# 24 column tiles of block 1's input projection multiplied ahead of the chain, in pairs by one level of a Strassen-type algorithm

## The chip, the core and the metric

The kernel runs on one core of a Trainium2 chip. The metric is the time of one execution on the device in microseconds (us), as the median of several runs. A core has five engines that run side by side: PE (TensorE, the matrix array), DVE (VectorE), ACT (ScalarE), POOL (GpSimd) and SP (SyncE, which here only issues DMA transfers). Each engine works through its own list of instructions in order, and an instruction that waits holds up all that stands behind it on the same engine. A scheduler decides, when the kernel is built, in which order each engine's list is written.

## The reference, cut to what matters

There are two blocks of a network on one sequence of 1024 tokens with 1024 features. The change lies in block 1 alone:

```python
shift, scale, gate = split(silu(c) @ w_mod + b_mod)
hx = rmsnorm(x, norm_g) * (1 + scale) + shift           # [1024, 1024]
q, k, v, zA, lr, uB, zB, gA, gB = split(hx @ w_in)      # one big projection
o  = gated_linear_attention(q, k, v, decays(lr), s0)    # s0 from 256 context tokens, 4 heads, two directions
yA = (rmsnorm(o) * silu(zA)) @ w_branch_a
yB = (pool(uB) * silu(zB)) @ w_branch_b                 # pool: differences of window sums, 4 groups
x  = x + gate * ((sigmoid(gA) * yA + sigmoid(gB) * yB) @ w_out)
```

Block 2 (attention with 16 heads and a feed-forward part) follows and is the same in both kernels.

## The kernel before, in words

Activations lie features first, in 8 tiles of 128 x 1024. Every product is made in three passes: each operand is split into a high and a low part (`split`: a cast on ACT, a subtraction on DVE or POOL), and `mm3` (lines 235 to 238) issues low x high, high x low, high x high as three matmuls of 128 x 512. For a weight tile `load` (line 226) reads 256 KB into `wraw` on SP's queue, ACT casts it to `whi` (line 190) and POOL subtracts to get `wlo` (line 182).

The front loads x, sums its squares, makes shift and scale by `mod` (a product with w_mod, a copy `row` on ACT, then four small products with `sel` that turn the row into columns `modv`), and forms the normed input in `hh`/`hl`: for each feature tile, x times scale on DVE, hh on ACT (line 423), hl on DVE. `gemm_late` starts the first two q products with feature tiles 0 to 3, while tiles 4 to 7 are still being made.

The projection is cut into column tiles: q, k, v, lr, and 40 "z" tiles (`proj_z`): 8 each of ub, zb, za, gb and ga. One z tile is 2 halves of tokens x 8 feature tiles x 3 = 48 matmuls, then for zb, za, gb, ga a sigmoid of three ACT functions on each half (lines 222 to 224). Results go to DRAM.

The attention chain `gla_head` runs for 4 heads: prefix sums of the decays (`X`, with small products `wup`), seven levels of scores (`EQ`, `EK`, `Q` with `kx`; mostly DVE work), a chain of states (each step: a transposition of `kh` with `ident`, a copy `kt` on DVE, a product `v,kt`, an update `sx` on DVE), then the outputs (`osq`, `rr`, `ya`). Between heads stand the `pool_group`s: `pool_tile` makes window sums `win` of u on DVE and splits them to `dh`/`dl`, a small product follows, and `zb` is multiplied in and stored to `yb_d`. Pool groups 0 and 1 follow heads 1 and 2, groups 2 and 3 both follow head 3.

`weave` puts the projection's column tiles as fillers before the 122 steps of that chain, evenly. So PE works on a filler while DVE and ACT work on the chain. After the chain, `load_split` (line 786) reads `yb_d` back as `raw` through three `ld` buffers and splits it to `rh`/`rl` for the branch products.

## Time and profile before

| what | value |
| --- | --- |
| median of three runs | 2676.07 us (2675.43 to 2678.48) |
| span of the profiled execution | 2679.3 us, mean granted TensorE clock 0.985 |
| PE busy | 2549.1 us (95%), 14390 matmuls |
| DVE busy | 1505.9 us (56%) |
| ACT busy | 961.0 us (36%) |
| POOL busy | 809.5 us (30%) |
| part with front and woven chain | 0 to about 873 us |

The profiled execution has no time of its own beside its span. Busy shares are means over stages of different kinds: the first 873 us hold the chain and its fillers, the rest is branch products and block 2. A granted clock of 1.00 is 2.4 GHz, 0.50 is 1.2 GHz.

### The profile page before, as it was taken

To read this page: it belongs to the slowest core of one execution; us is meant where nothing else is said; L and a number is where in the kernel's file an instruction comes from. 1 tells how busy PE (TensorE), PEld (TensorE's weight loads), DVE (VectorE), ACT (ScalarE), POOL (GpSimd) and SP (SyncE) were. 2 spreads that over 40 slices of the span, in tenths; PEclk is the share of its full clock that TensorE was granted. 3 is DMA by queue.
4 is the path that set the end of the run, shared out by engine and by line. 5 is a ranking of instruction groups with operands and counts; after the bars stand their busy time and mean duration, and the time that the engine had idled before them with its cause. 6 is when DMAs were issued, how large, how long until landed. Compare 5 with 4: busy or idle time off the path is not lost. (4 is left out here: it accounts for less than half of the span.)

```text
span 2679.3 us, 36279 instructions
## 1 busy us (share of the span) xinstructions
PE 2549.1 (95%) x14390; PEld 2015.2 (75%) x14390; DVE 1505.9 (56%) x2190; ACT 961.0 (36%) x1634; POOL 809.5 (30%) x592
## 2 busy tenths in 40 slices
...
GB/s 256 125 74 108 86 158 85 151 111 101 145 80 146 196 193 110 118 103 155 127 127 127 113 77 114 124 105 28 40 49 49 48 48 48 47 48 48 48 48 75
DMA packets 109113, 270.55 MB, mean 101 GB/s; under 512 B 13600, under 2 KB 18592, under 8 KB 108944
## 3 DMA queue, kind: packets, MB, share of 16 engines
...
## 5 line engine op out<-in xcount | busy, mean ns | idle before, releaser
L182 POOL TENSOR_TENSOR wlo<-wraw,whi 128x512 fp32r<-128x512 f32 (+1 forms) x363 | 537.3, 1482 | 1639.2 <-ACT whi L190 1593.1
L190 ACT CAST whi<-wraw 128x512 fp32r<-128x512 f32 (+1 forms) x363 | 223.8, 617 | 709.4 <-PE pp L238 617.6
L236 PE MATMUL pp<-hl,whi 128*128 128x512 f32 (+1 forms) x768 | 312.1, 407 | 4.8 <-DVE hl L185 4.8
L237 PE MATMUL pp<-hh,wlo 128*128 128x512 f32 (+1 forms) x768 | 307.2, 400 | 0.4 <-POOL wlo L182 0.4
L238 PE MATMUL pp<-hh,whi 128*128 128x512 f32 (+1 forms) x768 | 306.4, 399 | 0.0
L238 PE MATMUL pp<-u3h,whi 128*128 128x512 f32 x688 | 271.4, 395 | 0.0
L237 PE MATMUL pp<-u3h,wlo 128*128 128x512 f32 x688 | 271.0, 394 | 0.0
L236 PE MATMUL pp<-u3l,whi 128*128 128x512 f32 x688 | 270.2, 393 | 0.0
L182 DVE TENSOR_TENSOR x<-x,pp 128x512 f32<-128x512 f32 (+1 forms) x184 | 121.5, 664 | 208.5 <-PE pp L238 208.5
L236 PEld LDWEIGHTS pp<-hl,whi 128*128 128x128 f32 (+1 forms) x768 | 144.9, 189 | 42.5 <-DVE hl L185 5.8
L237 PEld LDWEIGHTS pp<-hh,wlo 128*128 128x128 f32 (+1 forms) x768 | 144.8, 189 | 38.9 <-issue 6.1
L238 PEld LDWEIGHTS pp<-hh,whi 128*128 128x128 f32 (+1 forms) x768 | 144.9, 189 | 33.7 <-issue 0.4
L1028 DVE COPY pt<-pg 128x512 f32<-128x512 f32 (+2 forms) x192 | 101.0, 553 | 92.5 <-PE pg L1026 91.8
L237 PEld LDWEIGHTS pp<-u3h,wlo 128*128 128x128 f32 x688 | 129.0, 188 | 30.9
L236 PEld LDWEIGHTS pp<-u3l,whi 128*128 128x128 f32 x688 | 129.2, 188 | 30.3
L238 PEld LDWEIGHTS pp<-u3h,whi 128*128 128x128 f32 x688 | 129.1, 188 | 30.1
L236 PE MATMUL pp<-fl,whi 128*128 128x512 f32 (+1 forms) x368 | 142.0, 386 | 0.0
L238 PE MATMUL pp<-fh,whi 128*128 128x512 f32 (+1 forms) x368 | 141.4, 384 | 0.0
L237 PE MATMUL pp<-fh,wlo 128*128 128x512 f32 (+1 forms) x368 | 140.8, 383 | 0.0
L185 DVE SCALAR_TENSOR_TENSOR t<-p,vec,t 128x1023 f32<-128x1023 f32 x88 | 122.1, 1395 | 33.1 <-ACT t L1144 32.1
L237 PE MATMUL pp<-uh,wlo 128*128 128x512 f32 x336 | 139.2, 414 | 0.0
L236 PE MATMUL pp<-ul,whi 128*128 128x512 f32 x336 | 138.3, 412 | 0.0
(384 smaller groups left out, 5434.0 us busy)
## 6 DMA issues: line engine op xcount, KB each, us to landing
...
```

Source lines behind the costliest of these rows:

```text
L182: return (eng or nc.vector).tensor_tensor(out=o, in0=a, in1=b, op=op)
L185: return (eng or nc.vector).scalar_tensor_tensor(out=o, in0=a, scalar=s, in1=b, op0=op0, op1=op1)
L190: nc.scalar.copy(hi, src)
L236: nc.tensor.matmul(ps, ah, bl, start=first, stop=False)
L237: nc.tensor.matmul(ps, al, bh, start=False, stop=False)
L238: nc.tensor.matmul(ps, ah, bh, start=False, stop=last)
L1028: nc.vector.tensor_copy(o, ps[:, :w])
```

## The change

24 of the 40 z tiles (ub, zb, ga) are taken out of the fillers and multiplied before the chain starts. Two column tiles ct and ct+4 make a pair; with the two halves of features and the two halves of tokens a pair is a 2 x 2 by 2 x 2 block product, and it is made with 7 products instead of 8 (Winograd's form). Such a product is 4 feature tiles x 3 = 12 matmuls of 128 x 512. The sums of weights (`up_sum`) are formed on DVE, the sums of the normed input (`t_sum`, `t_parts`) once, on DVE, ACT and POOL, and they stay resident for all 12 pairs. `up_result` combines the products on DVE and ACT, and accumulates two of them in a bank with others where that serves.

All of this stage is pinned: the scheduler must leave it in the order in which it is written, on each engine. The stage has its own memory pools; new pools are opened after it, and the loads of the context, of the tables and of the first q weights come from them. The weave then has 31 fillers and two small ones instead of 55 and two.

```diff
-NSLOT, NF, NT, NLD, NH, NQT = 32, 3, 2, 3, 5, 5
+NSLOT, NFIRST, NF, NT, NLD, NH, NQT = 32, 16, 3, 2, 3, 5, 5
...
+PROJ = [(n, ct) for n in ("ub", "zb", "ga") for ct in range(4)]
+REST = [n for n in ("za", "gb", "ga") if (n, 0) not in PROJ]
+SEVEN = (1, 6, 2, 5, 7, 3, 4)
+EARLY = (1, 5, 2, 6, 7, 3, 4)
...
+    def pin(ins):
+        return tc.keep_in_program_order(ins) if pinned[0] else ins
...
-    get = psum_pool(es, pp=(HALF, 3), pg=(HALF, 5))
+    get = psum_pool(es, pp=(HALF, 8))
+    size["h"] = ("e", N_E)
...
+    wm = {blk: mod_load(blk, row) for blk in (1, 0)}
+    bank_rstd(acc, r)
...
+    def up_load(q):
+        n, ct = PROJ[q]
+        raws[q] = []
+        for c in (ct, ct + 4):
+            for j in range(2):
+                raws[q].append(seg("wr", "wr"))
+                dma(raws[q][-1], io[f"w_{n}"][c, j])
+    def up_sum(q, n):
+        a11, a12, a21, a22 = raws[q]
+        if (q, n) in sums:
+            return
+        if n in (5, 6):
+            sums[q, 5], sums[q, 6] = seg("s1", "ws"), seg("s2", "ws")
+            tt(sums[q, 5], a21, a22, ALU.add)
+            tt(sums[q, 6], sums[q, 5], a11, ALU.subtract)
+        elif n == 3:
+            sums[q, 3] = sums[q, 6]
+            tt(sums[q, 3], a12, sums[q, 6], ALU.subtract)
+        elif n == 7:
+            tt(a11, a11, a21, ALU.subtract)
+            sums[q, 7] = a11
+        else:
+            sums[q, n] = raws[q][{1: 0, 2: 1, 4: 3}[n]]
+    def up_parts(q, n):
+        wh, wl = seg("wh", "w", F32R), seg("wl", "w", F32R)
+        split(sums[q, n], wh, wl, nc.gpsimd)
+        wparts[q, n] = [x.rearrange("p (k c) -> p k c", k=4) for x in (wh, wl)]
...
+    def up_product(q, n):
+        wh, wl = wparts.pop((q, n))
+        key = {1: 1, 2: 1, 7: 7, 4: 7}.get(n, 6)
+        first = (q, key) not in banks
+        if first:
+            banks[q, key] = get("pp")
+        ps = banks[q, n] = banks[q, key]
+        for j in range(4):
+            th, tl = T[n][j]
+            mm3(ps, wh[:, j], wl[:, j], th, tl, first and j == 0, j == 3, True)
...
+    def up_result(q, n):
+        if q not in outs and n in (2, 7):
+            outs[q] = row("o"), row("o")
+        p, v = outs.get(q, (None, None))
+        b = banks[q, n]
+        u1 = part.get((q, 1))
+        if n == 1:
+            part[q, 1] = seg("p1", "e")
+            copy(part[q, 1], b)
+        elif n == 2:
+            copy(p[:, LOW], b)
+        elif n == 7:
+            tt(v[:, HIGH], part[q, "v"], b, ALU.add)
+        elif n == 3:
+            tt(p[:, HIGH], u1, b, ALU.add)
+        elif n == 4:
+            tt(v[:, LOW], part[q, "u"], b, ALU.add)
...
+    def up_rest(q, i):
+        n, ct = PROJ[q]
+        if i == 6:
+            for c, o in zip((ct, ct + 4), outs[q]):
+                dma(z_d[n][c], o)
+        if n == "ub" or i > 3:
+            return
+        x = outs[q][i // 2][:, (LOW, HIGH)[i % 2]]
+        if n == "zb":
+            o = seg("s", "e")
+            sigmoid(x, o)
+            tt(x, x, o, ALU.mult)
+        else:
+            sigmoid(x, x)
...
+    T = {n: [(hh[j + k0][:, half], hl[j + k0][:, half]) for j in range(4)] for n, k0, half in ((1, 0, LOW), (2, 4, LOW), (3, 4, HIGH))}
...
+    def normed(k):
+        pin(nc.vector.tensor_scalar(g1s[:, k], modv[:, KD + k], 1.0, V("norm_g", k), op0=ALU.add, op1=ALU.mult))
+        x, sh = xt[k], modv[:, k, 0:1]
+        stt(x, x, g1s[:, k, 0:1], r, ALU.mult, ALU.mult)
+        act(hh[k], x, AF.Identity, bias=sh)
+        stt(hl[k], x, sh, hh[k].bitcast(F32), ALU.add, ALU.subtract)
...
+    def t_parts(n, j):
+        src = {5: xt[j][:, LOW], 7: xt[j][:, HIGH], 6: xt[j + 4][:, HIGH], 4: xt[j + 4][:, LOW]}[n]
+        t = row("T", F32R)
+        split(src, t[:, LOW], t[:, HIGH], nc.gpsimd if j % 2 else None)
+        T[n].append((t[:, LOW], t[:, HIGH]))
+    early = [(q, n) for n in EARLY for q in range(2)]
+    order = early + [(q, n) for q in range(2, len(PROJ)) for n in SEVEN]
...
+    for b in range(2):
+        mod(2 * b + 1, modv[:, KD + 4 * b : KD + 4 * b + 4], wm[2 * b + 1], tag="pp")
+        mod(2 * b, modv[:, 4 * b : 4 * b + 4], wm[2 * b], tag="pp")
+        pinned[0] = True
+        if b == 0:
+            wm = {blk: mod_load(blk, row) for blk in (3, 2)}
+            for q in range(2):
+                up_load(q)
+        else:
+            tt(dsh, modv[:, 4:8, 0], modv[:, :4, 0], ALU.subtract)
+        for k in range(4 * b, 4 * b + 4):
+            normed(k)
+        for j in range(4 - 4 * b):
+            t_sum(5, j)
+            t_parts(5, j)
+        for s in range(2 * b, 2 * b + 2):
+            up_sum(*early[s])
+            up_parts(*early[s])
+    for s, (q, n) in enumerate(order):
+        i = s - 14 if s < 14 else s % 7
+        if s:
+            up_result(*order[s - 1])
+        for n_, at in ((6, 1), (7, 3), (4, 6)):
+            for j in range(2 * (s - at), 2 * (s - at) + 2):
+                if 0 <= j < 4:
+                    if n_ == 6:
+                        t_sum(7, j)
+                    if n_ != 7:
+                        t_sum(n_, j)
+                    t_parts(n_, j)
+        nxt = 2 if s == 8 else q + 1 if i == 0 and q + 1 < len(PROJ) else 0
+        if nxt:
+            up_load(nxt)
+        if s + 4 < len(order):
+            up_sum(*order[s + 4])
+        if s and s + 3 < len(order):
+            up_parts(*order[s + 3])
+        if q > 2:
+            up_rest(q - 1, i)
+        elif q == 2:
+            for q_ in range(2):
+                up_rest(q_, i)
+        up_product(q, n)
+    up_result(*order[-1])
+    for i in range(7):
+        up_rest(len(PROJ) - 1, i)
+    pinned[0] = False
+    es.close()
+    front.close()
+    front = ExitStack()
+    wpool, sb = main_pools(front, NFIRST)
+    es = ExitStack()
+    get = psum_pool(es, pp=(HALF, 3), pg=(HALF, 5))
+    state = {"gla": None}
+    hch, hcl, xct = [], [], []
+    rc, accc = qt("rc", w=LC), b1k("accc")
+    for i in range(2):
+        xct.append(b1k(f"xc{i}"))
+        nc.sync.dma_start(xct[i].rearrange("p (k t) -> p k t", k=4), ctxT[4 * i : 4 * i + 4].rearrange("k p t -> p k t"))
...
-    wm = {blk: mod_load(blk, b1k) for blk in (1, 0)}
-    wq = [load(io["w_qk"][h, i], 4, P) for h in range(2) for i in range(2)]
-    bank_rstd(acc, r)
-    for b in range(2):
-        mod(2 * b + 1, modv[:, KD + 4 * b : KD + 4 * b + 4], wm[2 * b + 1], last[1] if b else None)
-        mod(2 * b, modv[:, 4 * b : 4 * b + 4], wm[2 * b], last[3] if b else None)
-        if b == 0:
-            wm = {blk: mod_load(blk, b1k) for blk in (3, 2)}
-            for i in range(2):
-                xct.append(b1k(f"xc{i}"))
-                nc.sync.dma_start(
-                    xct[i].rearrange("p (k t) -> p k t", k=4), ctxT[4 * i : 4 * i + 4].rearrange("k p t -> p k t")
-                )
-        for k in range(4 * b, 4 * b + 4):
-            nc.vector.tensor_scalar(g1s[:, k], modv[:, KD + k], 1.0, V("norm_g", k), op0=ALU.add, op1=ALU.mult)
-            x, sh = xt[k], modv[:, k, 0:1]
-            stt(x, x, g1s[:, k, 0:1], r, ALU.mult, ALU.mult)
-            hh.append(b1k(f"hh{k}", F32R))
-            hl.append(b1k(f"hl{k}", F32R))
-            last.append(nc.scalar.activation(hh[k], x, AF.Identity, bias=sh))
-            stt(hl[k], x, sh, hh[k].bitcast(F32), ALU.add, ALU.subtract)
...
-    qb = gemm_late([wq[:2], wq[2:]], hh, hl, tags=['pg', 'pp'], k0=4)
     context()
-    fill = [(("q", h), lambda h=h: proj_q(h, qb[h])) for h in range(2)]
+    fill = [(("q", h), lambda h=h: proj_q(h)) for h in range(2)]
...
-    fill += [((n, c), lambda n=n, c=c: proj_z(n, c)) for c in range(KD) for n in ("ub", "zb")]
-    fill += [((n, c), lambda n=n, c=c: proj_z(n, c)) for n in ("za", "gb", "ga") for c in range(KD)]
+    fill += [((n, c), lambda n=n, c=c: proj_z(n, c)) for n in REST for c in range(KD)]
...
-        fill.insert(16 + 16 * b, (("gate", b), lambda b=b: gate_x(b)))
+        fill.insert(12 + 6 * b, (("gate", b), lambda b=b: gate_x(b)))
     fill = [(k, max(0, CH1 * (n - 3) // (len(fill) - 3)), f) for n, (k, f) in enumerate(fill)]
...
     es.close()
-
-    # branch products and the merge
+    front.close()
+    hold.close()
+    wpool, sb = main_pools(ctx, NSLOT)
```

**The front.** On DVE, at the start of the program: x is scaled (the rows `x<-x,g1s,r`, 128x1024), then hl is taken. Before:

```order
L185 SCALAR_TENSOR_TENSOR x_4_237<-x_4_237,g1s,r_275 128x1024
L185 SCALAR_TENSOR_TENSOR x_5_240<-x_5_240,g1s,r_275 128x1024
L185 SCALAR_TENSOR_TENSOR x_7_245<-x_7_245,g1s,r_275 128x1024
L185 SCALAR_TENSOR_TENSOR x_9_250<-x_9_250,g1s,r_275 128x1024
L185 SCALAR_TENSOR_TENSOR hl_64_394<-x_4_237,modv,hh_63_393 128x1024
L185 SCALAR_TENSOR_TENSOR hl_66_400<-x_5_240,modv,hh_65_399 128x1024
L182 TENSOR_TENSOR modv<-pg_426,vec 128x8
L418 TENSOR_SCALAR g1s<-modv,vec 128x2
L185 SCALAR_TENSOR_TENSOR hl_68_406<-x_7_245,modv,hh_67_405 128x1024
L185 SCALAR_TENSOR_TENSOR hl_70_412<-x_9_250,modv,hh_69_411 128x1024
```

and of the change, the first two feature tiles, and then the place where tile 4 follows on tile 3:

```order
L207 SCALAR_TENSOR_TENSOR x_3_236<-x_3_236,g1s,r_274 128x1024
L207 SCALAR_TENSOR_TENSOR hl_320<-x_3_236,modv,hh_312 128x1024
L521 TENSOR_SCALAR g1s<-modv,vec 128x2
L207 SCALAR_TENSOR_TENSOR x_4_239<-x_4_239,g1s,r_274 128x1024
L207 SCALAR_TENSOR_TENSOR hl_321<-x_4_239,modv,hh_313 128x1024
```

```order
L204 TENSOR_TENSOR T_419<-x_6_244,T_419 128x512
L204 TENSOR_TENSOR x_8_249<-x_8_249 128x512
L204 TENSOR_TENSOR modv<-pp_445,vec 128x8
L204 TENSOR_TENSOR modv<-pp_462,vec 128x8
L204 TENSOR_TENSOR dsh<-modv 128x4
L521 TENSOR_SCALAR g1s<-modv,vec 128x2
L207 SCALAR_TENSOR_TENSOR x_10_254<-x_10_254,g1s,r_274 128x1024
L207 SCALAR_TENSOR_TENSOR hl_324<-x_10_254,modv,hh_316 128x1024
```

Before, four scalings stood together ahead of the four subtractions; now each subtraction (which needs ACT's hh of the same tile) stands directly behind its scaling. The rows for tiles 4 to 7 stand behind the sums for operand T and behind both modv of the second pair of w_mod blocks. On PE the first products stand in the same way behind both of these w_mod blocks; the last rows of `mod` (line 413) and the first product:

```order
L413 MATMUL pp_445<-sel,row_443 128x2 x4
L402 MATMUL pp_451<-wm_370,st_81 32x512 x2
L402 MATMUL pp_451<-wm_372,st_81 32x512 x2
L402 MATMUL pp_451<-wm_374,st_81 32x512 x2
L402 MATMUL pp_451<-wm_376,st_81 32x512 x2
L413 MATMUL pp_462<-sel,row_460 128x2 x4
L268 MATMUL pp_501<-hl_320,wh_426 128x512
L269 MATMUL pp_501<-hh_312,wl_427 128x512
L270 MATMUL pp_501<-hh_312,wh_426 128x512
L268 MATMUL pp_501<-hl_321,wh_426 128x512
```

Before, the first product of tile 0 stood ahead of the last w_mod block, and tiles 0 to 3 and then 4 to 7 followed each other in one product.

**Behind the last Winograd-type product.** SP's queue of the change, where the stores of ga end and the loads for context, tables and q weights follow (`o` are the results of the last two pairs):

```order
L216 DMA ga_d_146<-o_2128 128x1024
L216 DMA ga_d_150<-o_2129 128x1024
L216 DMA ga_d_147<-o_2275 128x1024
L216 DMA ga_d_151<-o_2276 128x1024
L607 DMA xc_426_2368<-in_ctxT 128x4x256
L607 DMA xc_427_2370<-in_ctxT 128x4x256
L645 DMA cosT_2399<-in_con 128x1024
L646 DMA sinT_2400<-in_con 128x1024
L262 DMA wraw_2426<-in_w_qk 128x512
L262 DMA wraw_2432<-in_w_qk 128x512
```

and before, where these loads stood in the first 40 rows of the queue, behind w_mod alone:

```order
L350 DMA wm_385<-in_w_mod 128x1024
L414 DMA xc_61_387<-in_ctxT 128x4x256
L414 DMA xc_62_389<-in_ctxT 128x4x256
L428 DMA edge<-in_con 128x64
L437 DMA cosT_500<-in_con 128x1024
L438 DMA sinT_501<-in_con 128x1024
L231 DMA wraw_654<-in_w_lr 128x384
L231 DMA wraw_660<-in_w_lr 128x384
L231 DMA wraw_749<-in_w_qk 128x512
L231 DMA wraw_755<-in_w_qk 128x512
```

The PE rows at this place are the last product with T, the sum over the squares of the context (`accc,ones`), and the first q product:

```order
L269 MATMUL pp_2299<-T_678,wl_2279 128x512
L270 MATMUL pp_2299<-T_678,wh_2278 128x512
L618 MATMUL pg_2378<-accc_2367,ones 128x256
L268 MATMUL pp_2438<-hl_320,whi_2427 128x512
L268 MATMUL pp_2464<-hl_320,whi_2427 128x512
L269 MATMUL pp_2438<-hh_312,wlo_2428 128x512
L270 MATMUL pp_2438<-hh_312,whi_2427 128x512
```

All loads of the next stage moved from the start of the queue to a place behind the stores of this stage's last results.

**The end of the chain.** PE before, at the last pool group's product (`dl`, `dh`) and behind it:

```order
L237 MATMUL pg_7900<-dh_7799,wlo_7805 128x512
L238 MATMUL pg_7900<-dh_7799,whi_7804 128x512
L236 MATMUL pg_7908<-dl_7800,whi_7804 128x512
L237 MATMUL pg_7908<-dh_7799,wlo_7805 128x512
L238 MATMUL pg_7908<-dh_7799,whi_7804 128x512
L236 MATMUL pp_7958<-hl_64_394,whi_7919 128x512
L237 MATMUL pp_7958<-hh_63_393,wlo_7920 128x512
```

and of the change:

```order
L270 MATMUL pg_8288<-dh_8268,whi_8273 128x512
L268 MATMUL pg_8299<-dl_8269,whi_8273 128x512
L269 MATMUL pg_8299<-dh_8268,wlo_8274 128x512
L270 MATMUL pg_8299<-dh_8268,whi_8273 128x512
L268 MATMUL pg_8307<-dl_8269,whi_8273 128x512
L269 MATMUL pg_8307<-dh_8268,wlo_8274 128x512
L270 MATMUL pg_8307<-dh_8268,whi_8273 128x512
L268 MATMUL pp_8602<-rl_8541,whi_8591 128x512
```

Before, 216 further filler matmuls (with `hl`, `hh`) stood between the last `dl` product and the first branch product (`rl`, `rh`); now the branch products follow directly. Between the last `osq` product of head 3 and the last `dl` product there are 207 filler matmuls before and 76 now. In the same way PE has, between the last score product of a head (`Q,kx`) and the first transposition of its state chain (`ident,kh`), 3, 49 and 34 filler matmuls for heads 1, 2 and 3 before, and none now. SP's queue of the change at the same place:

```order
L944 DMA yb_d_166<-zb_8278 128x1024
L944 DMA yb_d_167<-zb_8297 128x1024
L995 DMA raw_8539<-yb_d_160 128x1024
L995 DMA raw_8545<-yb_d_161 128x1024
L995 DMA raw_8551<-yb_d_162 128x1024
L995 DMA raw_8557<-yb_d_163 128x1024
L995 DMA raw_8563<-yb_d_164 128x1024
L995 DMA raw_8569<-yb_d_165 128x1024
L995 DMA raw_8575<-yb_d_166 128x1024
L995 DMA raw_8581<-yb_d_167 128x1024
```

Before, the eight `raw` loads stood between loads and stores of fillers, the first two of them ahead of the last `yb_d` stores; now all eight stand behind these.

## Rows read from the trace of the kernel before

**Rows 1.** The page: span, and busy time with its share and instructions.

```profile
span 2679.3 us, 36279 instructions
PE 2549.1 (95%) x14390; PEld 2015.2 (75%) x14390; DVE 1505.9 (56%) x2190; ACT 961.0 (36%) x1634; POOL 809.5 (30%) x592
```

**Rows 2.** Busy time by stretch: from:to length, engines' busy us (instructions), clock, DMA.

```profile
46.50:62.00 15.50, 15.15 (x71) 11.88 (x69) 10.80 (x12) 7.31 (x8) 3.04 (x2) 0.99 0.06 17
...
534.40:570.00 35.60, 31.38 (x577) 24.49 (x577) 34.07 (x39) 21.29 (x29) 8.37 (x5) 0.94 0.24 75
570.00:624.70 54.70, 54.66 (x248) 40.87 (x249) 21.12 (x51) 19.05 (x31) 10.04 (x9) 0.98 0.39 126
...
808.50:872.50 64.00, 60.21 (x256) 47.52 (x256) 47.74 (x56) 29.15 (x45) 16.53 (x15) 1.00 0.43 153
...
2000.00:2050.00 50.00, 50.00 (x217) 40.55 (x217) 26.32 (x30) 11.72 (x14) 13.64 (x9) 1.00 0.16 48
```

**Rows 3.** Timeline of the front: start, length, engine, line; idle before and its releaser.

```profile
25.37 0.59 ACT L367 COPY row<-pg 128x512 f32<-128x512 f32 x1 [0.51 <-PE pg L359]
...
26.99 1.92 PE L359 MATMUL pg<-wm,st 128*32 128x512 f32 x16
...
29.68 1.05 PE L370 MATMUL pg<-sel,row 128*128 128x2 f32 x8 [0.76 <-ACT row L367]
...
31.44 0.16 DVE L182 TENSOR_TENSOR modv<-pg,vec 128x8 f32<-128x8 f32 x1
...
33.77 1.15 ACT L423 ACTIVATE hh<-x,modv 128x1024 fp32r<-128x1024 f32 x1 [3.11 <-DVE x L185]
...
42.27 2.48 DVE L185 SCALAR_TENSOR_TENSOR hl<-x,modv,hh 128x1024 fp32r<-128x1024 f32 x2
...
44.66 1.28 DVE L185 SCALAR_TENSOR_TENSOR x<-x,g1s,r 128x1024 f32<-128x1024 f32 x1
...
45.53 0.59 ACT L367 COPY row<-pg 128x512 f32<-128x512 f32 x1 [5.84 <-PE pg L359]
```

**Rows 4.** Timeline of POOL: weight splits at three places.

```profile
30.22 4.66 POOL L182 TENSOR_TENSOR wlo<-wraw,whi 128x512 fp32r<-128x512 f32 x2 [20.11 <-ACT whi L190]
...
144.78 11.30 POOL L182 TENSOR_TENSOR wlo<-wraw,whi 128x512 fp32r<-128x512 f32 x1 [8.94 <-ACT whi L190]
...
738.58 1.29 POOL L182 TENSOR_TENSOR wlo<-wraw,whi 128x512 fp32r<-128x512 f32 x1 [6.39 <-ACT whi L190]
```

**Rows 5.** Stretch 100 to 870, groups by shape: busy us, mean ns, idle before.

```profile
L190 ACT CAST whi<-wraw 128x512 fp32r<-128x512 f32 x99 | 61.0, 617 | 58.1 <-PE pp L238 39.3 <-DMA wraw<-in_w_qk 5.9 <-PE pg L238 5.9
...
L223 ACT ACTIVATE z<-z,onet 128x512 f32<-128x512 f32 x54 | 39.0, 722 | 0.7
...
L224 ACT ACTIVATE z<-z 128x512 f32<-128x512 f32 x54 | 34.0, 630 | 1.3
L222 ACT ACTIVATE z<-pp 128x512 f32<-128x512 f32 x55 | 32.8, 596 | 130.6 <-PE pp L238 121.5 <-PE pg L359 9.0
...
L182 DVE TENSOR_TENSOR z<-pp,z 128x512 f32<-128x512 f32 x32 | 21.9, 686 | 22.4 <-ACT z L224 22.4
```

**Rows 6.** Timeline in head 3: last score products, A, first transposition.

```profile
731.80 0.70 PE L592 MATMUL pg<-Q,kx 128*32 128x32 f32 x59
...
737.27 2.90 DVE L604 COPY_PREDICATED A<-lmask,sd 32x256 f32<-32x256 uint8 x4
...
740.42 0.27 PE L642 MATMUL pg<-ident,kh 128*128 128x128 f32 x1
```

**Rows 7.** Timeline of the chain's end: SP, DVE, ACT.

```profile
829.43 0.38 SPq L707 DMA_DIRECT2D u<-ub_d  x1
...
832.99 1.24 DVE L182 TENSOR_TENSOR win<-u 128x1039 f32<-128x1039 f32 x1 [2.94 <-DMA u<-ub_d]
...
868.88 1.23 DVE L182 TENSOR_TENSOR dl<-d,dh 128x1024 fp32r<-128x1024 f32 x1 [1.11 <-ACT dh L190]
...
894.63 1.05 ACT L190 CAST rh<-raw 128x1024 fp32r<-128x1024 f32 x1 [1.28 <-DMA raw<-yb_d]
```

110 lines of the change are left out of this document (76 added, 34 removed).

## The prediction, made before the result was known

> **What bounds the kernel now.** I read the page's busy times first: PE is busy 2549.1 of 2679.3 us, no other engine above 56% [rows 1]. Then the table of stretches, because that share is a mean. In block 2 and the branch products PE is simply full: 217 matmuls in 50.00 us from 2000 on, one per 0.230 us, and that is my price of a 128x512 matmul [rows 2]. (The duration that a single matmul's row shows is longer, since matmuls overlap; only the rate adds up.) In the woven part PE is nearly full too, but by the fillers' grace: from 570.00 to 624.70, a chain of states, it works 54.66 us while DVE works 21.12; from 534.40 to 570.00, the levels of a head, DVE works 34.07 of 35.60 us and PE 31.38; from 808.50 to 872.50, the end of the chain, PE 60.21 and DVE 47.74 of 64.00 [rows 2]. So there are two limits that lie on top of each other: PE's sum, and the chain's own length on DVE and ACT. Taking fillers out lowers the first and not the second. In the front PE is dense from 46.5 us (15.15 busy us in the next 15.50) [rows 2].
>
> The thing to see is therefore not what PE saves but where it will stand still. I go through the program in time.
>
> **The saving.** 24 tiles x 48 matmuls = 1152 become 84 products x 12 = 1008. 144 matmuls less at 0.230 us: **-33.2 us**. The added sums on DVE (about four of 128x512 per pair, 0.69 us by the nearest row) and the sigmoids on ACT (0.60 + 0.72 + 0.63 = 1.95 us per half tile, four halves per pair) [rows 5] lie beside 7 x 12 x 0.230 = 19.3 us of matmuls per pair, and so does POOL's one split per product (1.29 us alone [rows 4], against 2.76 us of matmuls). ACT's worst pair needs 7 casts at 0.62, two copies and four sigmoids, 13.4 us of 19.3. In its steady state the new stage is bound by PE; I cost the rest at nothing there, 0 to 3 us. What hides it is the buffers three products ahead.
>
> **The front.** The chain of the pinned order, from modv's arrival at 31.44 + 0.16 [rows 3]: each feature tile is scaling 1.28, hh on ACT 1.15, hl 2.48 / 2 = 1.24 [rows 3], with small steps and handovers 3.8 us. Before, these overlapped in fours; now they follow each other. Tiles 0 to 3: 31.6 + 15.2 = 46.8. Then four differences and two subtractions for T at 0.69 with ACT's casts between, 4.5: 51.3. ACT's list has the last T cast, two weight casts (0.62 each [rows 5]) and only then the two row copies that w_mod's second pair needs: 53.8. Copy to columns 1.05, the second w_mod product 1.92, copy 0.59, columns 1.05 [rows 3]: 58.4. The first two products stand behind this on PE (24 matmuls, 5.5 us, done by 65), and on DVE tiles 4 to 7 stand behind modv: another 15.2, 73.8. The third product needs a sum of weights made after them (0.69), its cast (0.62) and its split on POOL (1.29): dense from about 76.4. With 5.5 us of work already done that equals a dense start at 71, against 46.5 before: +24.5. In before, the row copy of the last w_mod block was done by 46.1 [rows 3], and `gemm_late` filled the rest.
>
> In the 12 products that follow (33 us) POOL has 20 splits: 26 us at 1.29. The trace shows splits of 2.33 each (4.66 for two) while DVE was at work, and one of 11.30 us [rows 4], so POOL may bind here: at 2.33 it would need 47 us, 14 more than PE. I take 3.5 of these 0 to 14, nearer to the low end, since DVE has gaps in this stage and buffers run ahead. Front in all: **+28** (22 to 38). The Trainium skill (SBUF — State Buffer, Who interferes with whom) says that a DVE instruction with two SBUF inputs and a GpSimd instruction that reads SBUF share a port pair as an exclusive lock, the later one blocked for the whole of the other. By that rule DVE's and POOL's times would add here, some 21 + 26 = 47 us, and the front would cost about 38; the rows with 2.33 and 11.30 us agree with it.
>
> **Behind the last product.** Its result is added (0.69), two more halves go through the sigmoid on ACT (2 x 1.95) [rows 5], and only then the last two stores are issued, at +4.6. SP's queue holds the context, the tables and the q weights behind these stores. A load takes 3.56 us from issue to use (829.43 to 832.99) [rows 7], the second one about 1 more; then two squares (about 1.15 each, as hh), three additions (about 2.3), and the sum over the context, which stands on PE ahead of the first q product. 4.6 + 0.8 + 4.6 + 1.2 + 2.3 = 13.5. PE has nothing else in its list. Before, these loads were issued in the first 40 us and hidden. **+13** (9 to 16).
>
> **In the weave.** Behind a head's last score product DVE must finish sd, kh, A before the first transposition: 732.50 to 740.42 in head 3, 7.9 us [rows 6]. Before, 49 and 34 fillers filled this in heads 2 and 3 (11.3 and 7.8 us), 3 in head 1, 48 in head 0. Now none in heads 1 to 3, and 38 narrow ones (about 4.6 us) in head 0. PE stands for about 7.9 + 7.8 + 0.7 + 3.3 = 19.7; I take **+18**, as DVE may be somewhat earlier without the fillers' work. The bounds: 5, if PE is behind DVE there anyway; 28, if the levels' start, with fewer fillers too, waits 4 us in two heads more. Between the steps of states 72 to 89 fillers remain (16.6 to 20.5 us), and I cost that at nothing.
>
> **The end of the chain.** From 808.50 to 872.50 PE's 60.21 us hold 207 fillers (47.6 us), so 12.6 us of its own [rows 2]. Now 76 fillers: 12.6 + 17.5 = 30.1. DVE's chain through two pool groups keeps its length, 64.0 less some waits for u behind fillers on SP (2.94 the longest [rows 7]): 58. PE stands 28 where it stood 3.8: **+24** (15 to 30).
>
> **Behind the chain.** dl ends at 870.1, the last rh of the reloads at 895.7 [rows 7]: 25.6 us, in which PE had 216 fillers. Now there are none, and all eight loads stand behind the last `yb_d` stores (about 4.5 us after dl). Three buffers, each turn 3.56 + 1.05 + 1.23 = 5.8, three turns 17.5: the last part comes at about +22. The first branch tile has 48 x 0.230 = 11 us of products to run as the parts come in. **+10** (6 to 14).
>
> **Sum.** -33.2 + 28 + 13 + 18 + 24 + 10 = +59.8 us. Nothing in the branch products or block 2 changes. The profiled span of 2679.3 lies 3.2 above the median of 2676.07, so all terms carry over to the median: **2736 us**. With all low ends +24 (2700), with all high ends +93 (2769).
>
> **The rivals.**
> - *The weave follows PE's sum alone.* If the chain runs ahead of PE wherever fillers leave, the three thin places (18, 24, 10) cost nothing, and only front and boundary count: -33.2 + 28 + 13 = +8, **2684**. For it: PE is busy 54.66 of 54.70 us in a chain of states. Against it: DVE's own 34.07 of 35.60 and 47.74 of 64.00 us [rows 2], which don't get shorter. Chance 0.13.
> - *The weave gets shorter than PE's sum says* (faster than before). The removed fillers also leave ACT (1.95 us per half), POOL and DVE's `z` (0.69); if their splits are what stretched the chain, as in the 11.30 us split on which PE waited [rows 4], the weave loses that stall and some more, about 20 us, and the thin places cost nothing: 2684 - 20 = **2664**. It decides once the weave is more than 8 us shorter than its PE work says. Against it: that stall stands beside score work of head 0, whose order is kept. Chance 0.10.
> - *POOL blocked by a dense DVE.* With fewer fillers DVE's gaps close; three more splits of some 11 us [rows 4] that PE waits for would give 2736 + 33 = **2769**. For it: 11.30 against 1.29 us for one and the same instruction. Against it: half of the splits have left the weave. Chance 0.12.
>
> The Trainium skill (Perfetto Trace Analysis, Optimization Strategy) advises interleaving regimes whose most-contended engine differs; this change takes a PE regime out of such a mix, which points the same way as my terms and gives no size.
>
> **How the numbers follow.** My forecast has 0.65, the rivals 0.13, 0.10, 0.12. A measurement here can tell about 0.2% (5.4 us). Faster by more than that: the second rival, 0.10, of which a little (0.01) falls within. Same: that, and part of the first rival and of low ends, 0.06. Slower: 0.85. The range goes from the first rival's 2684 to the third's, 2772; about 2 in 10 lie outside.
>
> **What would show it.** In the profile of the changed kernel: the first dense run of products from about 76 us (from 50 would prove the front wrong); 84 products at about 2.8 us each, ending near 305; a gap of PE of 9 to 16 us behind them; DVE busy and PE idle for some 8 us behind the scores of heads 2 and 3; PE busy about half of the last 58 us of the chain; and a thin PE for some 20 us behind the last `dl`. If PE is dense in the chain's last 60 us, or if the granted clock stays low long after each gap, the sum is wrong.

## The result, and the profile after

The changed kernel takes **2787.4 us** (median of 4 runs, 2783.91 to 2791.58) against 2675.75 us for the kernel before on the same chip: ratio 1.0419, 95% interval 1.0403 to 1.0434. It is 111.7 us slower. The forecast was 2736 us, slower by 60, with a range up to 2772: the sign was right, the size was not, and the time lies 15 us above the range.

The page of the profiled execution (span and engines' busy time) answers to [rows 1]:

```profile
span 2788.0 us, 36390 instructions
PE 2550.1 (91%) x14246; PEld 2013.1 (72%) x14246; DVE 1621.6 (58%) x2323; ACT 1003.0 (36%) x1696; POOL 869.6 (31%) x636
```

PE runs 144 matmuls less and is as long busy as before (2549.1). So two things happened: PE stands still for 108 us more, and its matmuls run at a lower granted clock in places. Where, the table of stretches shows (from:to, length, busy us with instructions of PE, PEld, DVE, ACT, POOL, granted clock, DMA share, GB/s), in the order of the program: front, stage, behind its last product, states of head 2, end of the chain, block 2.

```profile
63.00:80.00 17.00, 7.62 (x24) 5.70 (x22) 11.95 (x15) 5.08 (x5) 0.00 (x0) 0.70 0.00 0
80.00:100.00 20.00, 15.73 (x49) 11.15 (x49) 15.77 (x16) 9.83 (x19) 12.16 (x8) 0.80 0.00 0
100.00:120.00 20.00, 15.44 (x56) 11.47 (x57) 15.09 (x16) 6.20 (x11) 14.57 (x11) 0.89 0.28 79
...
160.00:180.00 20.00, 20.00 (x90) 16.57 (x89) 8.77 (x11) 5.97 (x10) 9.31 (x8) 1.00 0.31 106
...
320.00:340.00 20.00, 4.85 (x13) 3.35 (x12) 4.88 (x9) 8.74 (x14) 2.51 (x2) 0.59 0.57 202
...
770.00:815.20 45.20, 37.95 (x150) 24.55 (x145) 20.92 (x49) 11.73 (x20) 2.65 (x4) 0.77 0.23 80
...
964.80:1022.10 57.30, 34.77 (x123) 26.72 (x122) 43.63 (x55) 17.18 (x26) 9.50 (x12) 0.77 0.37 128
...
2120.00:2170.00 50.00, 50.00 (x217) 40.42 (x217) 30.30 (x34) 14.06 (x16) 13.92 (x11) 1.00 0.18 48
```

How to read it: a stretch counts every matmul that lies in it even in part, so the rate is taken from start to start. In the stage that is 0.2267 us a matmul (705 starts from 160 to 320), which makes 88 in 20 us of a full PE at clock 1.00; in block 2 it is 0.231 to 0.232 (216 starts in 50 us, before and after). The stretches from 63 to 120 show 24, 49 and 56. The states of head 2 [rows 2, the row from 570.00] had PE full at clock 0.98; now they run at 0.77 and PE's busy 37.95 us are not 37.95 us of full work.

The PE timeline (start, length, engine, line, operation; idle before and its releaser) gives the single waits: front (with the first and the last of the first 24 matmuls), behind the stage, three of the end of the chain, the first branch product.

```profile
54.62 1.65 PE L413 MATMUL pp<-sel,row 128*128 128x2 f32 x7 [21.42 <-ACT row L213]
...
62.49 0.77 PE L268 MATMUL pp<-hl,wh 128*128 128x512 f32 x1
...
70.24 0.39 PE L270 MATMUL pp<-hh,wh 128*128 128x512 f32 x1
80.19 0.80 PE L268 MATMUL pp<-T,wh 128*128 128x512 f32 x1 [9.57 <-ACT wh L213]
81.99 0.80 PE L269 MATMUL pp<-T,wl 128*128 128x512 f32 x1 [1.01 <-POOL wl L204]
...
96.78 0.50 PE L269 MATMUL pp<-hh,wl 128*128 128x512 f32 x1 [1.57 <-POOL wl L204]
...
335.78 1.22 PE L618 MATMUL pg<-accc,ones 128*128 128x256 f32 x2 [15.15 <-DVE accc L204]
...
995.04 0.79 PE L268 MATMUL pg<-dl,whi 128*128 128x512 f32 x1 [9.41 <-DVE dl L204]
...
1009.14 0.77 PE L268 MATMUL pg<-dl,whi 128*128 128x512 f32 x1 [9.01 <-DVE dl L204]
...
1018.13 0.79 PE L268 MATMUL pg<-dl,whi 128*128 128x512 f32 x1 [4.11 <-DVE dl L204]
...
1031.89 0.79 PE L268 MATMUL pp<-rl,whi 128*128 128x512 f32 x1 [8.30 <-DVE rl L204]
```

**A ledger.** Two marks lie in every trace: the first gate product of head 0 (`pg<-lrc,wup`; 126.8 us before, 417.4 after) and the first branch product (`pp<-rl,whi`; 923.2 and 1031.9). What a kernel loses ahead of head 0 is its first mark less 126.8 less the stage's matmuls at 0.2267 us. Between the marks the kernel before takes 796.4 us; what the weave loses is the fillers taken out (tiles x 48 x 0.230, the forecast's price) less what this time shrinks by. Saved is the difference of those two prices. The last two columns are the net at the second mark and the difference of the profiled spans; they agree within 6.4 us in every row, so behind the second mark little happens.

| kernel | stage matmuls | head 0 | branch | lost ahead | lost in the weave | saved | net | spans |
|---|---|---|---|---|---|---|---|---|
| after | 1008 | 417.4 | 1031.9 | 62.1 | 83.1 | 36.5 | 108.7 | 108.7 |
| e4 plain products | 1152 | 428.6 | 1040.4 | 40.6 | 80.4 | 3.8 | 117.2 | 117.1 |
| e5 none first | 0 | 156.2 | 959.8 | 29.4 | 7.2 | 0 | 36.6 | 34.8 |
| e11 four pairs, mended | 336 | 248.5 | 984.2 | 45.5 | 27.6 | 12.1 | 61.0 | 59.0 |
| e8 eight pairs, mended | 672 | 319.8 | 968.0 | 40.7 | 28.4 | 24.3 | 44.8 | 51.2 |
| e12 twelve pairs, mended | 1008 | 398.2 | 989.0 | 42.9 | 59.4 | 36.5 | 65.8 | 64.9 |
| e9 gates moved | 1008 | 415.0 | 1009.6 | 59.7 | 63.2 | 36.5 | 86.4 | 84.6 |
| e10 twenty pairs | 1680 | 567.9 | 1203.1 | 60.2 | 280.4 | 60.7 | 279.9 | 281.7 |

For after: 417.4 - 126.8 - 228.5 = 62.1; 265.0 - (796.4 - 614.5) = 83.1; 265.0 - 228.5 = 36.5. The forecast had 28 + 13 = 41 ahead, 18 + 24 + 10 = 52 in the weave, and 33.2 saved. So 21 us are missing ahead of head 0 and 31 in the weave, and 3 us more are saved.

By place, the weave's 83 us are (the time from mark to mark on PE, with the fillers in it deducted at their price, after against before): from a head's last score product to its first state product, four heads together, 10.0 against 8.5; the rest of the states 74.9 against 48.2; the levels 55.6 against 43.2; between the heads 51.2 against 41.7; the end of the chain 40.8 against 16.3; behind it 8.9 against 0.7; the outputs are equal.

### The profile page after: what moved, and what is told of

Same layout as the page of the kernel before. It is cut to its first block, busy times and chain, and to the rows that moved or that the text cites. A ratio compares the mean times of both kernels' runs of the same rounds, so it can differ in the third digit from the quotient of the medians.

```text
span 2788.0 us, 36390 instructions
## 1 busy us (share of the span) xinstructions
PE 2550.1 (91%) x14246; PEld 2013.1 (72%) x14246; DVE 1621.6 (58%) x2323; ACT 1003.0 (36%) x1696; POOL 869.6 (31%) x636
## 5 line engine op out<-in xcount | busy, mean ns | idle before, releaser
L204 POOL TENSOR_TENSOR wlo<-wraw,whi 128x512 fp32r<-128x512 f32 (+2 forms) x315 | 475.3, 1512 | 1464.8 <-ACT whi L213 1424.8
L213 ACT CAST whi<-wraw 128x512 fp32r<-128x512 f32 (+2 forms) x315 | 194.9, 619 | 685.1 <-PE pp L270 602.9
L268 PE MATMUL pp<-hl,whi 128*128 128x512 f32 (+1 forms) x400 | 164.8, 413 | 0.6 <-DVE z L204 0.6
L269 PE MATMUL pp<-hh,wlo 128*128 128x512 f32 (+1 forms) x400 | 163.3, 408 | 0.3 <-POOL wlo L204 0.3
L270 PE MATMUL pp<-hh,whi 128*128 128x512 f32 (+1 forms) x400 | 163.1, 408 | 0.0
L207 DVE SCALAR_TENSOR_TENSOR t<-p,vec,t 128x1023 f32<-128x1023 f32 x88 | 121.6, 1390 | 33.2 <-ACT t L1353 32.2
L268 PE MATMUL pp<-rl,whi 128*128 128x512 f32 x320 | 128.2, 402 | 8.6 <-DVE rl L204 8.3
L270 PE MATMUL pp<-uh,whi 128*128 128x512 f32 x336 | 135.9, 404 | 0.0
L270 PE MATMUL pp<-rh,whi 128*128 128x512 f32 x320 | 128.2, 401 | 0.0
```

Of the source, the lines that this page charges most:

```text
L204: return pin((eng or nc.vector).tensor_tensor(out=o, in0=a, in1=b, op=op))
L207: return pin((eng or nc.vector).scalar_tensor_tensor(out=o, in0=a, scalar=s, in1=b, op0=op0, op1=op1))
L213: return pin(nc.scalar.copy(o, x))
L268: pin(nc.tensor.matmul(ps, ah, bl, start=first, stop=False, skip_group_check=again))
L269: pin(nc.tensor.matmul(ps, al, bh, start=False, stop=False, skip_group_check=again))
L270: pin(nc.tensor.matmul(ps, ah, bh, start=False, stop=last, skip_group_check=again))
```

## The experiments

Each was timed in three rounds against the kernel before, whose median went from 2674.6 to 2677.5 us between rounds; differences of that size are not read. Unless a text says otherwise the edit is to the changed kernel.

**e4: the same stage with plain products.** Each pair has four plain products of 24 matmuls in place of seven of 12, and no operand sums; the pairs that go first and all fillers stay.

```diff
-    def up_sum(q, n):
...
-    def up_parts(q, n):
...
+    def up_product(q, c, h):
+        half = (LOW, HIGH)[h]
+        ps = banks[q, c, h] = get("pp")
+        for k in range(KD):
+            wh, wl = wparts[q, c, k // 4]
+            mm3(ps, wh[:, k % 4], wl[:, k % 4], hh[k][:, half], hl[k][:, half], k == 0, k == KD - 1)
```

> The same 24 tiles first, in the same pinned stage and memory, but with plain products: 96 matmuls per pair, no sums of weights or inputs. First theory (sums cost nothing beside PE, save for the front's T): 1152 x 0.2225 = 256 us of matmuls, a start some 10 us earlier in effect: the stage ends at about 332 instead of 321, 2798 us (2790 to 2808). Rival (the sums on DVE, ACT and POOL eat what the algorithm saves): the stage ends at 321 or earlier, 2787 us or less.

Measured 2800.85 us (2798.17 to 2807.82), ratio 1.0482 [1.0464, 1.0499]: 13.5 us slower than the changed kernel by the medians, 8.4 by the profiled spans. So the algorithm does save time, but much less than the 32.6 us of its 144 matmuls: by the ledger the plain stage loses 40.6 us ahead of head 0 and the changed one 62.1. Inside the stage a matmul comes every 0.2267 us in both. What differs is the start: without operand sums the plain stage has no lasting gap behind 71 us, and it ends at 327.7 against 320.6. The sums of operands and the splits that they need cost over 20 us there. The larger part of the loss comes from what was moved: e4 loses it too.

**e5: nothing first.** All 40 tiles are fillers again, in the order of before, and so are the gates' places; the pools, the pinned front and the late context loads of the change stay.

```diff
-PROJ = [(n, ct) for n in ("ub", "zb", "ga") for ct in range(4)]
+PROJ = [(n, ct) for n in () for ct in range(4)]
...
+    fill += [((n, c), lambda n=n, c=c: proj_z(n, c)) for c in range(KD) for n in ("ub", "zb")]
+    fill += [((n, c), lambda n=n, c=c: proj_z(n, c)) for n in ("za", "gb", "ga") for c in range(KD)]
...
-        fill.insert(12 + 6 * b, (("gate", b), lambda b=b: gate_x(b)))
+        fill.insert(16 + 16 * b, (("gate", b), lambda b=b: gate_x(b)))
```

> No tile is multiplied first: all 40 z tiles are fillers in the order of before, but the rest of the rearrangement stays (pinned serial norm of the 8 feature tiles, new memory pools behind it, loads for context, tables and q behind that). First theory (front and boundary cost by themselves, the weave is slow only when thin): the first q products are dense from about 74 us instead of 46.5, the weave as before: 2676 + 27 = 2703 us (2692 to 2715), the gaps at the chain's end as before (under 5 us). Rival (the smaller pool of the weave or its new pools slow the weave itself): gaps in the heads and at the end like those of the changed kernel, 2740 us or more.

Measured 2715.14 us (2712.41 to 2716.42), 1.014 [1.0123, 1.0157]: 39.6 slower than before, at the first theory's upper bound. 29.4 of it are the front and the late context (PE dense from 74.6 against 46.5), and one thing that I had not counted stands behind the chain. The timeline of SP's queue there:

```profile
949.53 0.33 SPq L676 DMA_DIRECT2D ga_d<-z  x1
951.38 1.55 SPq L262 DMA_DIRECT2D wraw<-in_w_bb  x2
953.02 1.33 SPq L956 DMA_DIRECT2D raw<-yb_d  x3
```

And PE's, at the first branch product:

```profile
959.81 0.80 PE L268 MATMUL pp<-rl,whi 128*128 128x512 f32 x1 [12.36 <-DVE rl L204]
```

Here 50.8 us of fillers do stand behind the last `dl`, and PE still waits 12.36 us: the reloads of `yb_d` are issued only behind the last filler's store, 55 us after `yb_d` itself was last stored (896.77). The change opens new pools for the branch products' buffers where the first ones close; that this holds the reloads back is read from the code and this queue, and no run changes the pools alone. In before the last reload was cast at 894.63 [rows 7], 28 us ahead of its use.

**e3: the front in fours.** Scaling, hh and hl each for four feature tiles before the next step; the second pair of w_mod directly behind the first four; operand sums last.

```diff
+    def normed4(ks):
+        for k in ks:
...
+            stt(xt[k], xt[k], g1s[:, k, 0:1], r, ALU.mult, ALU.mult)
+        for k in ks:
+            act(hh[k], xt[k], AF.Identity, bias=modv[:, k, 0:1])
+        for k in ks:
+            stt(hl[k], xt[k], modv[:, k, 0:1], hh[k].bitcast(F32), ALU.add, ALU.subtract)
```

> The front's DVE and ACT work in another order: four scalings, four hh, four hl together, w_mod's second pair directly behind the first four, sums for T last. First theory (the serial pinned front costs): DVE and ACT save 2 x 5 us of turns, PE's first product comes at about 52 instead of 63 us and the dense run at about 62 instead of 82; 2787 - 18 = 2769 us, all other gaps the same. Rival (POOL's splits bind the first 14 products, so an earlier start waits there): 8 us or less, 2779 to 2787 us.

Measured 2776.67 us (2774.87 to 2777.55), 1.0382 [1.0366, 1.0397]: 10.7 us won, between the two (14.9 by the profiled spans). The first product started at 52.57 instead of 62.49 us, the third at 64.70 instead of 80.19, and the stage ended at 303.5 instead of 320.6. Behind the third product PE waits for ACT and POOL in both kernels; here:

```profile
64.70 0.50 PE L268 MATMUL pp<-T,wh 128*128 128x512 f32 x1 [2.36 <-ACT wh L213]
67.58 0.80 PE L269 MATMUL pp<-T,wl 128*128 128x512 f32 x1 [2.38 <-POOL wl L204]
...
77.13 0.50 PE L269 MATMUL pp<-hh,wl 128*128 128x512 f32 x1 [1.13 <-POOL wl L204]
```

So the new order (three things moved at once: the feature tiles, w_mod's second pair and the operand sums) brings the third product 15.5 us forward. What is lost behind it stays: against a full PE 15.6 us up to the end of the stage here, 17.4 in the changed kernel.

**e6: the place behind the last product.** The two pairs with the cheapest results go last, the first q weights are loaded early, and q's products stand ahead of the sum over the context.

```diff
+PROJ = [("ub", 0), ("ub", 1)] + [(n, ct) for n in ("zb", "ga") for ct in range(4)] + [("ub", 2), ("ub", 3)]
...
+    wq = [[load(io["w_qk"][h, i], 4, P) for i in range(2)] for h in range(2)]
...
+    for h in range(2):
+        proj_q(h, gemm(wq[h], hh, hl))
```

> Only the place behind the last product is changed: two ub pairs (no sigmoid) come last, the q weights are loaded first, the two q tiles are multiplied ahead of the context's sums. First theory (PE waits there for the results' stores, then loads, then the sum over the context): the gap of 15.15 us falls to 7 or 8, 2787 - 8 = 2779 us. Rival (the gap is set by the release of the memory of the first stage): 2785 us or more.

Measured 2781.65 us (2778.51 to 2783.43), 1.0389 [1.0371, 1.0406]: 5.7 us won, less than the 8 expected. PE's wait at this place fell from 15.15 to 5.17 us:

```profile
324.52 0.80 PE L268 MATMUL pp<-hl,whi 128*128 128x512 f32 x1 [5.17 <-ACT whi L213]
```

**e7: useless matmuls in the gaps.** 56, 30 and 62 matmuls of 128x512, whose results nobody reads, where PE stands still: in the front, ahead of the third product, behind the last one.

```diff
+    def warm(n, a, b):
+        ps = get("pp")
+        for i in range(n):
+            pin(nc.tensor.matmul(ps, a[:, :P], b, start=True, stop=True, skip_group_check=True))
```

> Useless matmuls (56, 30 and 62 of 128x512, into banks that nobody reads) are put into three of PE's gaps: behind the third w_mod product, ahead of the third product, and behind the last product. They add 148 matmuls and fill gaps of 21, 10 and 15 us. First theory (PE runs at 1.2 GHz behind each gap, which costs 9.9 us from 60 to 140 and 2.5 us behind the boundary): the granted clock there rises to nearly 1.00, 2787 - 8 = 2779 us (2775 to 2784), in spite of more work. Rival (only the gaps cost, the clock does not matter): 2787 us or more.

Measured 2787.21 us (2784.99 to 2792.32), 1.0413 [1.0394, 1.0433]: nothing. The clock did rise, as two stretches of e7 show (columns as above):

```profile
60.00:75.00 15.00, 13.12 (x61) 10.65 (x60) 9.88 (x13) 3.91 (x4) 0.00 (x0) 1.00 0.00 0
...
325.00:330.00 5.00, 5.00 (x24) 4.14 (x23) 0.00 (x0) 0.81 (x1) 0.00 (x0) 1.00 1.02 326
```

The same stretches of the changed kernel:

```profile
60.00:75.00 15.00, 9.92 (x36) 7.90 (x32) 8.54 (x12) 4.04 (x4) 0.00 (x0) 0.73 0.01 1
...
325.00:330.00 5.00, 0.00 (x0) 0.00 (x0) 0.00 (x0) 0.37 (x1) 0.00 (x0) 0.50 0.74 237
```

But the third product came at 78.3 instead of 80.2 and the context's sum at 334.3 instead of 335.8: what ends these waits is DVE, ACT, POOL and the loads. My theory that the clock behind the gaps costs 8 us here fell.

**e9: the gates' two fillers two places earlier**, among scores instead of between the steps of the states.

```diff
-        fill.insert(12 + 6 * b, (("gate", b), lambda b=b: gate_x(b)))
+        fill.insert(10 + 6 * b, (("gate", b), lambda b=b: gate_x(b)))
```

> One table entry is changed: the two small fillers that make the gates (w_mod products with their own loads) go from places 12 and 18 of the list to 10 and 16, so that they stand among the scores of heads 1 and 2 instead of between their states. Theory (in the states the chain waits for their loads, the row copy and the columns, 783.4 to 794.1 in head 2, and goes on at half clock): some 10 us in each of the two heads, 2787 - 20 = 2767 us (2760 to 2775). Rival (the state chain lasts longer because fillers ran out, and the gates only filled its gaps): 2780 us or more.

Measured 2768.2 us (2765.65 to 2768.86), 1.0344 [1.0329, 1.036]: **19.2 us won by one number.** What it takes away shows in the changed kernel's states of head 2, first in the timeline of PE:

```profile
776.83 0.70 PE L854 MATMUL pg<-vc,kt 128*128 128x256 f32 x2 [3.75 <-DVE kt L852]
...
780.24 1.22 PE L854 MATMUL pg<-v,kt 128*128 128x256 f32 x2 [0.56 <-DVE kt L852]
781.25 0.42 PE L850 MATMUL pg<-ident,kh 128*128 128x128 f32 x1
782.23 1.22 PE L854 MATMUL pg<-v,kt 128*128 128x256 f32 x2 [0.56 <-DVE kt L852]
783.38 3.63 PE L402 MATMUL pg<-wm,st 128*32 128x512 f32 x12
788.77 1.92 PE L402 MATMUL pg<-wm,st 128*32 128x512 f32 x4 [1.76 <-DMA wm<-in_w_mod]
...
792.50 1.70 PE L413 MATMUL pg<-sel,row 128*128 128x2 f32 x8
794.06 0.45 PE L850 MATMUL pg<-ident,kh 128*128 128x128 f32 x1
```

The timeline of DVE in the same stretch:

```profile
783.49 0.48 DVE L207 SCALAR_TENSOR_TENSOR sx<-sx,ec,pg 128x256 f32<-128x256 f32 x1 [1.31 <-PE pg L854]
...
794.24 0.17 DVE L204 TENSOR_TENSOR gate<-pg,vec 128x8 f32<-128x8 f32 x1 [4.68 <-PE pg L413]
794.55 0.29 DVE L852 COPY kt<-pg 128x128 f32<-128x128 f32 x1
```

And the one DMA on SP's queue:

```profile
785.35 0.33 SPq L216 DMA_DIRECT2D wm<-in_w_mod  x1
```

From 783.49 to 794.55 no step of the chain is done. The gate's product (L402) waits for its second weights, issued only at 785.35, because SP waited 15.5 us for PE's earlier L402 to free the buffer; behind it on PE's queue stands the next transposition (L850, 794.06). The kernel before had a gate in the states of head 2 as well, with 121 fillers (27.8 us) around it, and lost nothing; here the chain itself waits. The states of heads 1 and 2, the fillers' time deducted, took 27.3 and 29.6 us; in e9 13.0 and 18.0 (14.2 and 13.9 before). Some 7 us are given back where the second gate now stands: the levels of head 2 take 24.6 us beside their fillers instead of 17.5. (The changed list has 31 entries with the two gates among them, before it had 55 with them; the section on the change counts the gates twice.)

**e1, e8, e11, e12: fewer pairs, and the mended parts together.** e1 leaves `ga` to the fillers. e8 is e1 with e3 and e6. e11 has the four `ub` pairs alone, e12 all twelve, both with e3 and e6 and with the gates out of the states.

```diff
+PROJ = [(n, ct) for n in ("ub", "zb") for ct in range(4)]
```

> ga goes back into the weave: 8 pairs first instead of 12, 39 fillers instead of 31. First theory (the loss lies in PE's gaps in the thinned weave and in the half clock in and behind them): 4 x 12 x 0.2225 = 10.7 us more matmuls, but the gaps at the chain's end and behind it (22.5 + 8.3 us, and 9.4 us of clock) go nearly all, and more than half of the gaps (31 us more than before) and of the clock loss in the heads: about 2735 us (2720 to 2755). Rival (the new stage itself is what costs, the weave goes by PE's sum): 2787 + 11 = 2798 us less nothing.

> 8 pairs first (ga back in the weave), the front in fours, and the boundary with ub last and q ahead of the context. If the parts add: 2749 - 11 - 8 = 2730 us (2722 to 2738), still above the kernel before, since what 8 pairs save (96 x 0.23 = 22 us) is less than front and boundary still cost. Rival (parts overlap): 2740 us or more.

> 4 pairs first (ub), 32 z tiles in the weave, with the front in fours and the boundary with q ahead of the context. Between 0 pairs (2715) and 8 pairs (2749, mended 2730) the unmended value should be about 2732, the mended one 17 less: 2715 us (2706 to 2722), above the kernel before, since 4 pairs save 48 x 0.23 = 11 us and the front, the boundary and the reload behind the chain still cost more. Rival (with few pairs the weave stays full and the saving shows): 2690 us or less.

> The changed kernel with its 12 pairs and all three mends: front in fours, boundary with ub last and q first, gates among the scores. If the parts add: 2787 - 11 - 6 - 20 = 2750 us (2742 to 2760); the rest, 75 us above before with 33 us saved, is then the thin chain (its end 24, behind it 9, heads some 30), and what is left of front and boundary (about 40). Rival (mends in the front and weave hide each other): 2765 us or more.

Measured: e1 2748.71 us (2746.3 to 2751.28), 1.0278 [1.0263, 1.0294]; e8 2730.18 (2727.84 to 2732.22), 1.0195 [1.0175, 1.0214]; e12 2748.25 (2746.01 to 2752.82), 1.0274 [1.0258, 1.0289]. The parts add up: 10.7 + 5.7 + 19.2 = 35.6 from e3, e6 and e9 against 39.2 in e12. But e1's 38.7 us are not the pairs' alone: with 8 more fillers in the list the gates land outside the states by themselves, and the states of heads 1 and 2 take 11.0 and 10.6 us beside their fillers. The pairs' own share shows in e8 against e12, where the gates are out of the states in both: 18.1 us. e1 also tells the end of the chain apart from what is behind it. With 202 fillers at the end PE loses nothing there (16.7 us of its own, 16.3 before); behind it PE waits 12.4 us with 77 fillers, against 8.9 with none in the changed kernel.

e11 missed: 2742.34 (2739.56 to 2745.02), 1.0252 [1.0235, 1.0269], 20 us above the expected range. By the ledger, ahead of head 0 it loses 45.5 where e8 loses 40.7, and in the weave 28, as e8 does: with fewer pairs the fixed costs stay and only the saving shrinks, from 24 to 12 us. I had expected the weave's loss to go with the pairs. Of e11's 28 us, 11.4 are the wait for the reloads behind the chain, the same as in e5 (11.3) and e8 (11.8); it does not depend on the pairs, and no run here mends it. The rest is spread over several places, 6 us at the most; why they stay there is open.

**e2, e10: more and less for the weave.** e2 keeps the twelve pairs and computes the four `ga` tiles a second time as fillers (88 us of useless PE work). e10 does all 20 pairs first and puts the gates behind the last head.

```diff
-REST = [n for n in ("za", "gb", "ga") if (n, 0) not in PROJ]
+REST = ["za", "gb", "ga"]
```
```diff
+PROJ = [(n, ct) for n in ("ub", "zb", "ga", "za", "gb") for ct in range(4)]
```

> The changed kernel, with the 8 ga tiles computed a second time as fillers of the weave: 384 matmuls of useless work, 88 us at 0.230. First theory (the weave's gaps are there for want of fillers): the time rises by far less than 88, by 88 less the gaps and clock loss that they fill (up to 31 + 27 in gaps, 35 in clock): 2800 to 2825 us. Rival (the weave goes by PE's sum, the loss is elsewhere): 2787 + 88 = 2875 us.

> All 40 z tiles first, as 20 pairs: 96 matmuls (21 us) less than with 12 pairs, no z filler left in the weave, the gates behind the last head. Theory (the weave now follows the chain's own length): the stage grows by 8 x 84 x 0.2225 = 150 us, the weave loses 177 us of fillers but gets only some 60 us shorter: 2787 + 150 - 60 = 2877 us (2850 to 2890). Rival (PE's sum): 2787 - 21 = 2766 us.

e2: 2828.09 us (2822.8 to 2833.16), 1.0575 [1.0559, 1.0591], 3 us above the range. Of 88 us of added work only 40.7 show against the changed kernel. Part of this is the gates again, which the longer list puts outside the states; against e9, where they are outside too, 59.9 show. So some 28 us fill gaps, and the rival by which the weave follows PE's sum (2875) is refuted. e10: 2963.4 us (2962.72 to 2964.51), 1.1076 [1.1059, 1.1093], 73 us above the range. Between the two marks it needs 635.2 us where the changed kernel needs 614.5, with 177 us of fillers (16 tiles) less. The weave got **longer** by losing work. By place, the states got shorter (155 against 170 us in all), and so did the levels (129 against 138). What got longer lies between the heads: from the last output product of head 1 to the first score product of head 2 81.3 us against 53.0, and from head 2 to head 3 70.0 against 53.0. The first long wait there is PE's for the pool group's `dl`, and all of the next head's v, k and q stand behind it; among these PE waits 11.5 us more for one weight split on POOL (12.43 us from 873.44):

```profile
820.60 0.77 PE L268 MATMUL pg<-dl,whi 128*128 128x512 f32 x1 [14.67 <-DVE dl L204]
```

Between heads 2 and 3 the wait for `dl` is 15.94 us. This is read from the trace; no run tests it.

**e13, e14: useless matmuls in that thinned weave.** To e10, e13 adds three matmuls of 128x512 between the transposition and the product of every step of the states, e14 eight ahead of each level of the scores; their order on PE is fixed.

```diff
+    def warm(n, get):
+        ps = get("pp")
+        for i in range(n):
+            keep(nc.tensor.matmul(ps, hh[i][:, :P], hh[i][:, :HALF], start=i == 0, stop=i == n - 1, skip_group_check=True))
...
+            keep(nc.tensor.transpose(pt[:, :P], kd[:, c * P : c * P + P], ident))
+            warm(3, get)
```

> All 20 pairs first, and three useless matmuls of 128x512 between the transposition and the product of every step of the states (18 steps a head, 72 in all, 216 matmuls, 48 us of PE work). Theory (a chain of states left without fillers runs at half clock, and that lengthens it): with all pairs first the states of head 3 took 39.3 us at clock 0.50, a step 1.99 us; in the kernel after the change they took 32.7 with 19.6 us of fillers, a step 1.46. So each head's states get 5 to 6.6 us shorter although 12 us of work are added: 2943 us (2935 to 2952). Rival (the chain's own work on DVE sets the step, the clock only shows that PE is idle): no gain, 2960 or more.

> All 20 pairs first, and eight useless matmuls of 128x512 ahead of each of the seven levels of a head's scores (224 matmuls, 50 us of PE work). Theory (the levels are bound by DVE and ACT, which work 27.9 and 15.4 of head 3's 33.8 us while PE's own work there is 9.1 us; fillers or clock change nothing): 2963 us, 2957 to 2972. Rival (half clock costs here as well, up to half of 9.1 us per head): 2945.

e13: 2972.6 us (2969.5 to 2973.05), 1.1103 [1.1086, 1.1119]; e14: 2922.09 us (2920.12 to 2926.34), 1.0919 [1.0901, 1.0938]. Both totals went against the theory, and head 3, which has no filler in either kernel, tells why. The stretches of head 3's levels and states in e10:

```profile
1042.50:1076.30 33.80, 9.07 (x479) 8.22 (x480) 27.93 (x34) 15.43 (x19) 9.73 (x6) 0.50 0.21 64
1076.50:1115.80 39.30, 24.44 (x56) 12.56 (x52) 17.10 (x43) 1.34 (x2) 0.00 (x0) 0.50 0.00 1
```

The same two in e13:

```profile
1068.10:1097.00 28.90, 9.09 (x480) 8.23 (x480) 27.35 (x35) 14.75 (x16) 0.14 (x2) 0.50 0.12 38
1097.20:1129.10 31.90, 27.18 (x106) 17.54 (x103) 17.10 (x43) 1.32 (x2) 0.00 (x0) 0.84 0.00 1
```

The states: 39.3 us at clock 0.50 alone, **31.9 us with 12 us of useless work** at 0.84, and DVE's 17.10 us the same. One step, from product to product, was 1.99 us in e10 and became 1.46. PE's timeline in e10, then in e13:

```profile
1086.89 1.22 PE L854 MATMUL pg<-v,kt 128*128 128x256 f32 x2 [0.56 <-DVE kt L852]
1087.90 0.42 PE L850 MATMUL pg<-ident,kh 128*128 128x128 f32 x1
1088.88 1.22 PE L854 MATMUL pg<-v,kt 128*128 128x256 f32 x2 [0.56 <-DVE kt L852]
```

```profile
1108.00 0.68 PE L863 MATMUL pg<-v,kt 128*128 128x256 f32 x2
1108.52 0.27 PE L858 MATMUL pg<-ident,kh 128*128 128x128 f32 x1
1108.55 0.94 PE L725 MATMUL pp<-hh 128*128 128x512 f32 x3
1109.46 0.70 PE L863 MATMUL pg<-v,kt 128*128 128x256 f32 x2
```

The order of the chain's own instructions is the same in both, so in states without fillers the clock is part of the price, in head 3 as my theory had it: 7.4 of 39.3 us. The total of e13 rose since the fixed order drove real fillers and useless ones into the states of heads 0 to 2 together (46 us each, PE busy 41.48 of 46.20 in head 2). The levels: DVE is busy in 27.35 of 28.90 us at clock 0.50, so they are bound by DVE's chain, as expected (in e14, with useless matmuls ahead of each level, 28.1). In e10 they took 33.8, because on ACT a cast of a branch weight waited for its load and held up the `EQ` behind it, for which DVE then waited. The timelines of ACT and DVE in e10:

```profile
1050.28 0.62 ACT L213 CAST whi<-wraw 128x512 fp32r<-128x512 f32 x1 [7.13 <-DMA wraw<-in_w_bb]
...
1051.89 1.44 DVE L204 TENSOR_TENSOR EQ<-EQ,q 128x1024 f32<-128x1024 f32 x1 [5.36 <-ACT EQ L768]
```

e14's 41 us came from elsewhere: its fixed order pushed the real fillers out of the levels into the states, where heads 0 to 2 then took 32.4, 33.1 and 32.3 us with some 21 us of fillers each, against 36.2, 38.4 and 37.5 with 5 or less. That makes 14 us; the rest lies in the places that the fillers left. That reading rests on the two traces; a run that moves the fillers alone was not made.

## Why the prediction was wrong

**The saving** was right as far as it goes: in the stage's steady state the sums lie beside the matmuls, one per 0.2267 us with them (after) and without (e4). The price of 0.230 is a little low for block 2, since 217 matmuls in 50 us count two that lie in it in part; from start to start it is 0.231 to 0.232.

**The front was mis-sized**: +28 forecast, 45.6 measured. (The stage ends at 320.6; 1008 x 0.2267 before that is 92.1, against 46.5.) Up to the third product the chain of the pinned order held: it came at 80.19 where I had 76.4, a loss of 28.2 against 24.5. **The step that failed** is the term for what follows: "I take 3.5 of these 0 to 14". Measured are 17.4 us, above even the upper end: "dense from about 76.4" did not hold. The first 24 matmuls were done by 70.63, PE then waited 9.57 us, and from 80.19 to 120 it started 105 where a full PE has 176. The mechanism was not the one I feared either. POOL's splits took 1.27 to 1.75 us each, not 2.33, and POOL was busy 26.7 of the 40 us; ACT's casts waited for DVE's sums, POOL for ACT's casts and PE for both, one behind the other: 8.6 of the 16 us lost from 80.19 to 120 are PE's waits for them, the rest is the lower clock (0.84 on the mean). e7 filled the gap ahead of the third product, and by 120 us it was 4 matmuls ahead. The buffers did not run far enough ahead to hide this chain. e4, without the sums, loses nothing after 80 us.

**Behind the last product** +13 forecast, 15.15 measured: right, and e6 shows that 5.7 can be had back.

**In the weave** the sum had +18 between a head's last score and its states; measured is 10.0 against 8.5 us, next to nothing. I had counted on no fillers there, but in heads 1 to 3 there are 36, 12 and 21 between the first transposition and the first state product (3.75 us of waiting are left at 776.83 in head 2). The step that failed is "Between the steps of states 72 to 89 fillers remain (16.6 to 20.5 us), and I cost that at nothing": measured are 74.9 against 48.2 us, 26.7 more. This is the gates' fillers, whose places in the list are numbers that the change left to fall among fewer fillers, a term that the sum did not have. With them moved (e9, e12) the steps of the states take 44 us beside their fillers, less than before: without the gates the nothing would have been right, and nothing is left for the half clock of head 2's steps to explain. Also missing from the sum are the levels, 12.4 us, and the stretches between the heads, 9.5. The upper bound of 28 had levels that wait 4 us in two heads more; heads 1 and 2 lost 5.0 and 4.2. Why is not shown.

**The end of the chain** +24 forecast, 24.5 measured (40.8 against 16.3 us beside the fillers): right, and so was its working, DVE's length less what PE has to do. e1, with its 202 fillers there, loses nothing.

**Behind the chain** +10 forecast, 8.2 measured (8.9 against 0.7 us beside the fillers): right in size, but by luck. PE waits there 8.9 us with no filler, 12.4 with 77 (e1) and 12.0 with 221 (e5), for reloads that stand behind the last store. The missing fillers are not what causes it.

**The rivals.** The weave by PE's sum alone (2684) falls with e2 and e10. A shorter weave (2664) did not come: the levels of heads 1 to 3 take 38.9, 36.8 and 34.0 us against 32.5, 35.3 and 33.7. POOL blocked in the weave did not come: the one long wait in head 0 was 12.54 us before and is 11.13 now. (The third rival's own sum is 2769; the range's end of 2772, said to be the third's, is not worked out.)

The Trainium skill (TensorE: Matmul & The Clock Gate, "Loop structure matters more than you think") says that the loop nest decides whether matmuls stay warm, that is at the full clock, with long waits between them as the bad case. The states of head 3 agree, 39.3 us at clock 0.50 against 31.9 at 0.84. In the gaps of e7 the clock rose as well, and the time stayed the same.

No kernel here beats the one before; the best, e5, has no Strassen-type product at all, and its 36.6 us are lost to the pinned front, the late loads and the reloads behind the chain. With all three parts mended (e12) the change still loses 42.9 + 59.4 and saves 36.5.
